# Gate matrices made one token at a time on VectorE and GpSimd, and S of 96 e-tiles computed ahead instead of 64

## The chip, the cores and the metric

The program runs on one core of a Trainium2 chip. TensorE does the matmuls, VectorE (DVE in the rows) and GpSimd (POOL) elementwise work, ScalarE (ACT) activations and copies out of PSUM, SyncE (SP) issues most DMAs; GpSimd also issues the indirect ones. The metric is the device time of one execution in microseconds. The kernel before took 2036.5, 2039.18 and 2039.2 us in three runs, median 2039.18. The profiled execution took 2032.77 us, with a span of 2030.9 us from its first instruction to its last.

## The reference

The block is one layer on 512 tokens of width 1024: adaLN, a dilated-window and a differential attention branch, a merge, and at the end a PEER layer. Only the PEER layer matters here. For every token it picks 128 of 16384 single-neuron experts (8 heads with 16 each, from two top-16 lists of 128 keys) and adds up their outputs:

```
eidx = e1 * PEER_N_KEYS + e2
gate = jax.nn.softmax(top, axis=-1)
u = expert_u[eidx]
vv = expert_v[eidx]
act = jax.nn.gelu(jnp.einsum('td,thkd->thk', xc, u).astype(jnp.float32), approximate=False)
wts = (gate * act).astype(xc.dtype)
return jnp.einsum('thk,thkd->td', wts, vv)
```

## The kernel before

**Two ways for the experts.** The tokens are four groups of 128. Group 0 is done sparsely: for each of its 128 slots one indirect DMA on GpSimd's queue (`gather`, line 1056) brings a row of `expert_u` per token, VectorE takes the dot product (`dot`, line 1062, op at L1064), and a second gather brings the row of `expert_v`, which VectorE adds with its weight (`add`, line 1071, op at L1076). These 256 gathers share four buffers (`GB`), so a gather waits for the VectorE op that frees its buffer. The other three groups, 384 tokens, are done densely over all 16384 experts, in 128 e-tiles of 128 experts.

**Dense path, S.** For an e-tile, `gelu_s` (line 872) loads 512 KB of `uT`, ScalarE makes its rounded part (L91) and VectorE or GpSimd the rest (L92, tile `wlo`), TensorE does 24 matmuls of 384 columns into `pj` (L86 to L88, 8 of each), and ScalarE applies gelu into `am` (L879). The first `NS` e-tiles are done ahead of the main loop by `run_ahead` and stored in DRAM (`gls`); the others are done live, inside the main loop.

**Dense path, gate matrices.** Each of the 384 tokens needs a 128x128 matrix of its gates (16384 experts), which is a product of two one-hot factors. The stage at lines 1092 to 1152 makes it in 96 steps of `T` = 4 tokens, 32 steps for each token group. In a step VectorE compares two index rows with `iota` (`oh0`, `oh1`, L1125), multiplies `oh0` by the high and by the low half of the gates (`og0`, `og1`, L1130), all four as 128x512 operations on f16; TensorE does 8 matmuls with `oh1` (L1137, tile `pg`), two for each token; ScalarE copies the result into `stage` (L1139). After 8 steps four DMAs write it to DRAM (`gd`, L1146). Tiles `oh` and `og` have three buffers each, `pg` two.

**The main loop** (lines 1196 to 1223) goes over the 128 e-tiles in chunks of 8. A chunk of 8 live e-tiles takes turns with a chunk of 8 that were done ahead (order d a d a ...). `stage_s` runs 4 tiles ahead (`LEAD`): it loads `gch`, 1536 KB per chunk from `gd`, and either loads `am` from `gls` (L1168) or computes it. Then VectorE multiplies `am` by the gates (L1201), ScalarE and VectorE split it into `ah` and `al`, the 512 KB of `expert_v` are loaded and split (on GpSimd for one tile in four), and TensorE does 18 matmuls of 512 columns into `y` (L1220). Jobs of the sparse path are handed out along the way; `J0` = 48 of them belong to the gate stage, and a live tile gets twice the share of one done ahead.

**What sets the order.** Each engine works through its own queue in order. The queues come from a scheduler that goes by its own estimates, so instructions of the gate stage, of S and of the sparse jobs are woven together there; GpSimd's main-loop part keeps the order written.

## Time and profile before

| what | value |
|---|---|
| median of three runs | 2039.18 us |
| profiled execution, its span | 2032.77 us, 2030.9 us |
| TensorE busy | 1911.0 us (94%) |
| VectorE busy | 1589.5 us (78%) |
| ScalarE, GpSimd busy | 847.8 us (42%), 854.3 us (42%) |
| attention, projections, first S tiles and selection | 0 to about 923 us |
| gate stage: first `pg` matmul to last | 923.5 to 1213 us |
| TensorE idle until the first `y` matmul | 1213 to 1227 us |
| main loop: first `y` matmul to last | 1227.7 to 2023.5 us |

Busy time is an average over stages, so each stage is read by itself. In a timeline, matmuls overlap and their ends are modelled: the pace is the distance between two starts.

### The profile page before, as it was taken

What the parts mean: (1) busy time and instruction counts of PE and PEld (TensorE: products, weight loads), DVE (VectorE), ACT (ScalarE), POOL (GpSimd) and SP (SyncE); (2) the same over time, 40 slices, a digit from 0 to 9 for tenths busy, and PEclk for the clock granted to TensorE, in tenths of its full rate; (3) what the DMA queues carried; (4) which work ended last, traced back from release to release, by engine and by line L of the source; (5) the groups of instructions that cost most, each with busy time, mean ns of one, the idle gap of its engine ahead of it and who ended that gap; (6) DMA issues with size and microseconds to landing.
All of it is one profiled execution on the core that took longest, in us unless ns stands there. A gap on an engine that the chain in (4) does not pass through costs nothing.

```text
span 2030.9 us, 28280 instructions
## 1 busy us (share of the span) xinstructions
PE 1911.0 (94%) x9858; PEld 1658.5 (82%) x9858; DVE 1589.5 (78%) x3212; ACT 847.8 (42%) x1330; POOL 854.3 (42%) x598
## 2 busy tenths in 40 slices
PE   6999999989899899999999968999999999999998
PEld 5987777777777788999999946888888888888886
DVE  7488585886766669999888885777879797777887
ACT  3444345656533333345555652333333333333331
POOL 2554332352244531021442313465657464646553
PEclk9999999999999899999999958999999999999999
DMA  7344142132146421577788767888888788878886
GB/s 260 94 125 115 53 146 58 37 94 88 54 150 213 142 72 54 163 268 267 277 305 295 253 251 250 296 313 292 320 291 331 283 323 303 307 289 303 308 305 218
DMA packets 197200, 434.71 MB, mean 214 GB/s; under 512 B 16273, under 2 KB 95426, under 8 KB 196930
## 3 DMA queue, kind: packets, MB, share of 16 engines
q1 hardware_dynamic: 159376, 296.55, 43.2%
q0 software_dynamic: 36864, 134.23, 18.2%
q10 hardware_dynamic: 818, 2.12, 0.3%
q8 instruction: 77, 1.26, 0.2%
q14 instruction: 65, 0.53, 0.1%
HBM read 390.90 MB, written 41.94 MB: 213 GB/s over the span
## 4 chain that ended last, share of the span: by engine, by line
PE 47%; DVE 16%; DMA 9%; issue 5%; POOL 1%; ACT 1%; SPq 0%; DVEq 0%; POOLq 0%; ACTq 0%
PE y L1220 18%; PE pj L86 8%; PE pj L87 7%; PE pj L88 7%; PE pg L1137 3%; DMA gat<-expert_u,eidx 2%; DMA gat<-expert_v,eidx 2%; DVE wlo L92 2%; DMA raw<-uT 1%; DMA raw<-w_ada 1%; DVE mr L933 1%; DVE acc L1076 1%; DVE idx L935 1%; DMA raw<-expert_v 1%; DVE oh L1125 1%
## 5 line engine op out<-in xcount | busy, mean ns | idle before, releaser
L91 ACT ACTIVATE whi<-raw 128x1024 fp32r<-128x1024 f32 (+3 forms) x431 | 384.7, 896 | 520.4 <-DMA raw<-expert_v 142.9
L92 POOL TENSOR_TENSOR wlo<-raw,whi 128x1024 fp32r<-128x1024 f32 (+2 forms) x156 | 332.5, 2135 | 557.3 <-ACT whi L91 534.2
L92 DVE TENSOR_TENSOR wlo<-raw,whi 128x1024 fp32r<-128x1024 f32 (+3 forms) x275 | 310.5, 1131 | 115.1 <-ACT whi L91 114.5
L88 PE MATMUL pj<-h2h,wlo 128*128 128x384 f32 x1008 | 344.2, 342 | 4.1 <-DVE wlo L92 4.1
L86 PE MATMUL pj<-h2h,whi 128*128 128x384 f32 x1008 | 343.5, 341 | 0.5 <-ACT am L879 0.5
L87 PE MATMUL pj<-h2l,whi 128*128 128x384 f32 x1008 | 343.3, 341 | 0.0
L1058 POOL DMA_INDIRECT gat<-expert_u,eidx x128 | 162.1, 1266 | 254.9 <-DVE rkt L1015 102.2
L1220 PE MATMUL y<-whi,ah 128*128 128x512 f32 x768 | 248.0, 398 | 16.2 <-ACT ah L91 16.2
L1058 POOL DMA_INDIRECT gat<-expert_v,eidx x128 | 188.9, 1476 | 143.6 <-DVE acc L1076 83.6
L1220 PE MATMUL y<-wlo,ah 128*128 128x512 f32 x768 | 245.4, 397 | 0.0
L1220 PE MATMUL y<-whi,al 128*128 128x512 f32 x768 | 236.1, 398 | 7.8 <-DVE al L92 7.7
L1076 DVE SCALAR_TENSOR_TENSOR acc<-gat,wts,acc 128x1024 f32<-128x1024 f32 x127 | 188.9, 1488 | 43.3 <-DMA gat<-expert_v,eidx 43.0
L86 PE MATMUL pj<-whi,hh 128*128 128x512 f32 (+2 forms) x512 | 190.8, 386 | 10.7 <-DVE gA L651 4.4
L1064 DVE SCALAR_TENSOR_TENSOR gscr<-gat,h2tok 128x1024 bf16<-128x1024 f32 x128 | 176.1, 1376 | 27.3 <-DMA gat<-expert_u,eidx 27.0
L87 PE MATMUL pj<-wlo,hh 128*128 128x512 f32 (+2 forms) x512 | 194.9, 381 | 2.3 <-DVE wlo L92 2.3
L88 PEld LDWEIGHTS pj<-h2h,wlo 128*128 128x128 f32 x1008 | 191.1, 190 | 5.2 <-DVE wlo L92 4.8
L86 PEld LDWEIGHTS pj<-h2h,whi 128*128 128x128 f32 x1008 | 191.0, 190 | 4.5 <-ACT am L879 1.4
L87 PEld LDWEIGHTS pj<-h2l,whi 128*128 128x128 f32 x1008 | 191.0, 189 | 2.5
L88 PE MATMUL pj<-whi,hl 128*128 128x512 f32 (+2 forms) x512 | 190.5, 379 | 0.0
L1220 PEld LDWEIGHTS y<-whi,ah 128*128 128x128 f32 x768 | 144.2, 189 | 46.4 <-ACT ah L91 17.2
L1220 PEld LDWEIGHTS y<-whi,al 128*128 128x128 f32 x768 | 144.2, 189 | 46.4 <-DVE al L92 11.6
L1220 PEld LDWEIGHTS y<-wlo,ah 128*128 128x128 f32 x768 | 145.1, 189 | 35.2
(313 smaller groups left out, 3213.3 us busy)
## 6 DMA issues: line engine op xcount, KB each, us to landing
raw<-uT SPq DMA_DIRECT2D x128, 512.0 KB, 4.3
raw<-expert_v SPq DMA_DIRECT2D x128, 512.0 KB, 5.4
gd<-stage SPq DMA_DIRECT2D x48, 512.0 KB, 5.2
gch<-gd SPq DMA_DIRECT2D x16, 1536.0 KB, 10.9
raw<-w_in SPq DMA_DIRECT2D x88, 256.0 KB, 2.7
raw<-w_ada SPq DMA_DIRECT2D x64, 256.0 KB, 2.9
am<-gls SPq DMA_DIRECT2D x64, 192.0 KB, 8.2
gls<-am SPq DMA_DIRECT2D x62, 192.0 KB, 3.8
```

Source lines behind the costliest of these rows:

```text
L86: nc.tensor.matmul(ps, lh, rh, start=start, stop=False)
L87: nc.tensor.matmul(ps, lh, rl, start=False, stop=False)
L88: nc.tensor.matmul(ps, ll, rh, start=False, stop=stop)
L91: nc.scalar.activation(hi, raw, AF.Copy)
L92: (eng or nc.vector).tensor_tensor(lo, raw, hi.bitcast(F32), op=OP.subtract)
L933: nc.vector.match_replace(out=r, in_to_replace=v[:, 0:8], in_values=s, imm_value=-3.0e38)
L935: nc.vector.max_index(out=i[:, 8:16], in_max=v[:, 8:16], in_values=r)
L1058: nc.gpsimd.indirect_dma_start(out=t, out_offset=None, in_=src, in_offset=bass.IndirectOffsetOnAxis(ap=eidx[:, s:s + 1], axis=0))
L1064: nc.vector.scalar_tensor_tensor(scr, t, 1.0, h2tok, op0=OP.mult, op1=OP.mult, accum_out=act[:, s:s + 1])
L1076: nc.vector.scalar_tensor_tensor(acc, t, wts[:, s:s + 1], acc, op0=OP.mult, op1=OP.add)
L1137: nc.tensor.matmul(p[:, j * 128:j * 128 + 128], oh[1][:, :, q + j], pcs[i][:, :, q + j], start=i == 0, stop=i == 1)
L1220: nc.tensor.matmul(ys[b][n], l[:, bs], r[:, n * 512:n * 512 + 512], start=n_ == 0 and i == 0, stop=n_ == 127 and i == 2)
```

## The change

The value `NS` goes from 64 to 96. In the chunk order this makes one live chunk followed by three done ahead (d a a a, four times). In the gate stage one comparison and two products of a step are replaced by one operation per token and half, which compares `line` (0 to 127) with the token's first index and multiplies by the token's gate half, both taken as one scalar per partition. VectorE does this for the high half, GpSimd for the low half; the results lie contiguously for each token. The second comparison (`oh`) stays as it was.

```
-    ND, NS = 384, 64
+    ND, NS = 384, 96
...
+    line = gt.tile([128, 128], HF, name="line")
+    nc.vector.tensor_copy(line, ioti)
...
-            s = gt.tile([128, 128], HF if n < 2 else F32, name=f"sT{n}", bufs=2)
+            s = gt.tile([128, 128], HF if n == 1 else F32, name=f"sT{n}", bufs=2)
...
+        gh16 = gt.tile([128, 128], HF, name="gh16", bufs=1)
+        nc.vector.tensor_copy(gh16, tr[2])
+        gp = [gt.tile([128, 128], F32, name="gp", bufs=2), tr[2]]
+        nc.vector.tensor_copy(gp[0], gh16)
+        nc.vector.tensor_tensor(gp[1], tr[2], gp[0], op=OP.subtract)
...
-            oh = []
-            for i in range(2):
-                o = gt.tile([128, 128, T], HF, name=f"oh{i}", bufs=OB)
-                nc.vector.tensor_tensor(o, tr[i][:, None, ts].to_broadcast([128, 128, T]), iota, op=OP.is_equal)
-                oh.append(o)
-            pcs = []
-            for i in range(2):
-                o = gt.tile([128, 128, T], HF, name=f"og{i}", bufs=OB)
-                nc.vector.tensor_tensor(
-                    o, oh[0], gp[i][:, None, ts].to_broadcast([128, 128, T]), op=OP.mult)
-                pcs.append(o)
+            oh = gt.tile([128, 128, T], HF, name="oh", bufs=OB)
+            nc.vector.tensor_tensor(oh, tr[1][:, None, ts].to_broadcast([128, 128, T]), iota, op=OP.is_equal)
+            pcs = [gt.tile([128, T, 128], HF, name=f"og{i}", bufs=OB) for i in range(2)]
+            for j in range(T):
+                tj = slice(t0 + j, t0 + j + 1)
+                nc.vector.tensor_scalar(pcs[0][:, j], line, tr[0][:, tj], gp[0][:, tj], op0=OP.is_equal, op1=OP.mult)
+                nc.gpsimd.tensor_scalar(pcs[1][:, j], line, tr[0][:, tj], gp[1][:, tj], op0=OP.is_equal, op1=OP.mult)
...
-                        nc.tensor.matmul(p[:, j * 128:j * 128 + 128], oh[1][:, :, q + j], pcs[i][:, :, q + j],
+                        nc.tensor.matmul(p[:, j * 128:j * 128 + 128], oh[:, :, q + j], pcs[i][:, q + j, :],
```

On TensorE's queue, this is the place before where the last S matmul of the gate stage stands (`pj`), and then the end of the stage:

```order
L86 MATMUL pj<-h2h,whi 128x384
L87 MATMUL pj<-h2l_6198,whi 128x384
L88 MATMUL pj<-h2h,wlo 128x384
L1137 LDWEIGHTS oh_10291
L1137 MATMUL pg<-og_10293,oh_10291 128x128
...
L1137 MATMUL pg<-og_11055,oh_11051 128x128
L1220 MATMUL y_12372<-whi,ah 128x512
```

Behind these rows the matmuls of S have run out, and only gate steps follow up to the first `y`. The same place now (lines after the edit are three lower):

```order
L87 MATMUL pj<-h2l_6198,whi 128x384
L88 MATMUL pj<-h2h,wlo 128x384
L1134 LDWEIGHTS oh
L1134 MATMUL pg<-og_11173,oh 128x128
...
L1134 MATMUL pg<-og_11434,oh 128x128
L1217 MATMUL y_13846<-whi,ah 128x512
```

Before, 26 of the 96 steps stand behind the last S matmul, now 8. In front of the first `pg` matmul stand about 27.5 S tiles before and 28 now; in front of the first `y` matmul 70 before and 102 now (in both, six of them are the first live tiles).

On GpSimd's queue, the end of the gate stage before had only gathers of the sparse path (`gat`) and splits of main-loop weights (`wlo`):

```order
L92 TENSOR_TENSOR wlo_12385<-raw_12387,whi_12386 128x1024
L1058 DMA gat_11067<-expert_u,eidx_8063 128x1024
L92 TENSOR_TENSOR wlo_12451<-raw_12453,whi_12452 128x1024
L92 TENSOR_TENSOR wlo_12519<-raw_12521,whi_12520 128x1024
L1058 DMA gat_12579<-expert_u,eidx_8063 128x1024
```

None of these is waited for by the gate steps. Now the low halves of the last 8 steps (`og1`, four tokens in a row) stand between gathers:

```order
L1058 DMA gat_14194<-expert_v,eidx_8063 128x1024
L1129 TENSOR_SCALAR og1_11203<-line_8074,sT0_10401,sT2_10409 128x128 x4
L1129 TENSOR_SCALAR og1_11225<-line_8074,sT0_10401,sT2_10409 128x128 x4
L1129 TENSOR_SCALAR og1_11250<-line_8074,sT0_10401,sT2_10409 128x128 x4
L1058 DMA gat_14197<-expert_v,eidx_8063 128x1024
L1058 DMA gat_14200<-expert_v,eidx_8063 128x1024
L1129 TENSOR_SCALAR og1_11306<-line_8074,sT0_10401,sT2_10409 128x128 x4
L1129 TENSOR_SCALAR og1_11331<-line_8074,sT0_10401,sT2_10409 128x128 x4
L1058 DMA gat_14265<-expert_v,eidx_8063 128x1024
L1129 TENSOR_SCALAR og1_11353<-line_8074,sT0_10401,sT2_10409 128x128 x4
L1058 DMA gat_14268<-expert_v,eidx_8063 128x1024
L1058 DMA gat_14304<-expert_v,eidx_8063 128x1024
```

Each of these gathers waits for a buffer, and the `og1` behind it waits with it. VectorE's queue over the same 8 steps now reads, in its second half:

```order
L1076 SCALAR_TENSOR_TENSOR acc_8065<-gat_14123,wts_8067,acc_8065 128x1024
L1076 SCALAR_TENSOR_TENSOR acc_8065<-gat_14126,wts_8067,acc_8065 128x1024
L1128 TENSOR_SCALAR og0_11305<-line_8074,sT0_10401,gp_10413 128x128 x4
L1123 TENSOR_TENSOR oh_11303<-sT1_10405,iota_8072 128x512
L1128 TENSOR_SCALAR og0_11330<-line_8074,sT0_10401,gp_10413 128x128 x4
L1123 TENSOR_TENSOR oh_11328<-sT1_10405,iota_8072 128x512
L1076 SCALAR_TENSOR_TENSOR acc_8065<-gat_14129,wts_8067,acc_8065 128x1024
L1128 TENSOR_SCALAR og0_11352<-line_8074,sT0_10401,gp_10413 128x128 x4
L1076 SCALAR_TENSOR_TENSOR acc_8065<-gat_14194,wts_8067,acc_8065 128x1024
L1123 TENSOR_TENSOR oh_11350<-sT1_10405,iota_8072 128x512
L1076 SCALAR_TENSOR_TENSOR acc_8065<-gat_14197,wts_8067,acc_8065 128x1024
L1076 SCALAR_TENSOR_TENSOR acc_8065<-gat_14200,wts_8067,acc_8065 128x1024
```

Before, no add of the sparse path stood between the last 11 steps on VectorE's queue. In the main loop, VectorE's queue has 9 to 11 dots and adds per eight e-tiles of a chunk done ahead before, and now 9 to 13 with one of 17; of a live chunk 15 to 17 before and 17 to 20 now.

## Rows read from the trace of the kernel before

**Rows 1.** The page: TensorE's busy time, and the chain by engine.
```profile
PE 1911.0 (94%) x9858; PEld 1658.5 (82%) x9858; DVE 1589.5 (78%) x3212; ACT 847.8 (42%) x1330; POOL 854.3 (42%) x598
...
PE 47%; DVE 16%; DMA 9%; issue 5%; POOL 1%; ACT 1%; SPq 0%; DVEq 0%; POOLq 0%; ACTq 0%
```

**Rows 2.** Busy time by stretch (start:end length, engines, clock, DMA share, GB/s), gate stage.
```profile
923.00:1130.00 207.00, 207.00 (x1326) 195.66 (x1325) 183.01 (x375) 110.56 (x135) 65.68 (x36) 1.00 0.80 280
1130.00:1213.00 83.00, 68.97 (x476) 60.42 (x473) 74.59 (x172) 52.54 (x55) 26.76 (x14) 0.77 0.71 250
...
1213.00:1227.00 14.00, 0.00 (x0) 0.00 (x0) 0.49 (x2) 0.33 (x1) 0.00 (x0) 0.50 0.93 311
```

**Rows 3.** The same stretches, line L1137 alone (TensorE, its loads).
```profile
1130.00:1213.00 83.00, 46.46 (x332) 35.91 (x329) 0.77 0.71 250
923.00:1130.00 207.00, 64.69 (x439) 45.73 (x440) 1.00 0.80 280
```

**Rows 4.** The same stretches, line L86 alone, 8 matmuls per S tile.
```profile
1130.00:1213.00 83.00, 16.68 (x48) 9.22 (x48) 0.77 0.71 250
923.00:1130.00 207.00, 100.62 (x293) 55.68 (x293) 1.00 0.80 280
```

**Rows 5.** Timeline of TensorE in S (start, length, instruction).
```profile
1119.52 0.34 PE L86 MATMUL pj<-h2h,whi 128*128 128x384 f32 x1
...
1120.56 0.34 PE L86 MATMUL pj<-h2h,whi 128*128 128x384 f32 x1
```

**Rows 6.** Timeline of VectorE near the end of the gate stage.
```profile
1198.47 1.78 DVE L1125 TENSOR_TENSOR oh<-sT,iota 128x512 f16<-128x512 f16 x5
1200.14 1.45 DVE L1130 TENSOR_TENSOR og<-oh,gp 128x512 f16<-128x512 f16 x4
```

**Rows 7.** Groups by form: 128x128 operations with scalars (busy, mean ns, idle before).
```profile
L349 POOL TENSOR_SCALAR ropeS<-ropeS 128x128 f32<-128x128 f32 x4 | 1.1, 296 | 0.0
...
L757 POOL TENSOR_SCALAR ob<-ob,r 128x128 f32<-128x128 f32 x8 | 3.8, 491 | 6.3 <-DVE r L103 6.3
...
L1015 DVE TENSOR_SCALAR rkt<-rb 128x128 f32<-128x128 bf16 x4 | 0.9, 214 | 0.0
```

**Rows 8.** Timelines of GpSimd and VectorE in the main loop.
```profile
1481.90 3.57 POOL L92 TENSOR_TENSOR wlo<-raw,whi 128x1024 fp32r<-128x1024 f32 x1
...
1483.11 3.44 DVE L1076 SCALAR_TENSOR_TENSOR acc<-gat,wts,acc 128x1024 f32<-128x1024 f32 x1
...
1488.08 1.27 DVE L1076 SCALAR_TENSOR_TENSOR acc<-gat,wts,acc 128x1024 f32<-128x1024 f32 x1
```

**Rows 9.** Busy time by stretch in the main loop, columns as in rows 2.
```profile
1296.00:1328.00 32.00, 32.00 (x163) 29.05 (x162) 20.72 (x25) 11.74 (x16) 17.46 (x9) 1.00 0.72 269
...
1353.00:1386.00 33.00, 33.00 (x144) 26.61 (x143) 26.72 (x28) 10.97 (x15) 20.90 (x12) 1.00 0.99 364
...
1759.00:1795.00 36.00, 34.54 (x150) 27.71 (x150) 31.07 (x39) 12.21 (x16) 17.55 (x14) 1.00 0.99 369
...
1780.00:1790.00 10.00, 10.00 (x45) 8.04 (x44) 8.75 (x12) 4.12 (x5) 4.77 (x4) 1.00 1.04 402
```

**Rows 10.** One of these stretches, line L1220 alone.
```profile
1353.00:1386.00 33.00, 32.81 (x142) 26.25 (x141) 1.00 0.99 364
```

**Rows 11.** DMA issues (KB each, median us to landing).
```profile
raw<-expert_v SPq DMA_DIRECT2D x128, 512.0 KB, 5.4
...
gch<-gd SPq DMA_DIRECT2D x16, 1536.0 KB, 10.9
...
am<-gls SPq DMA_DIRECT2D x64, 192.0 KB, 8.2
...
gat<-expert_v,eidx POOLq DMA_INDIRECT x128, 7.4
```

**Rows 12.** VectorE's waits, 1250 to 2000 us (total, times, longest).
```profile
DVE acc L1076 <- DMA gat<-expert_v,eidx: 43.0, 27, 5.1
...
DVE am L1201 <- DMA am<-gls: 19.7, 8, 4.9
```

**Rows 13.** The page: the gathers' issue on GpSimd.
```profile
L1058 POOL DMA_INDIRECT gat<-expert_v,eidx x128 | 188.9, 1476 | 143.6 <-DVE acc L1076 83.6 <-DVE gscr L1064 22.7 <-DVE acc L1074 10.0
```

More of the change, by code (lines that the diff above doesn't have):

```diff
@@ L1105, in peer @@
             nc.tensor.transpose(p[:, :128], t, ident)
-            s = gt.tile([128, 128], HF if n < 2 else F32, name=f"sT{n}", bufs=2)
+            s = gt.tile([128, 128], HF if n == 1 else F32, name=f"sT{n}", bufs=2)
             nc.scalar.activation(s, p[:, :128], AF.Copy, scale=1.0 if n < 2 else GS)
             tr.append(s)
-        gT = tr[2]
-        gp = []
-        for i in range(2):
-            q = gt.tile([128, 128], HF, name=f"gp{i}", bufs=2)
-            nc.vector.tensor_copy(q, gT)
-            if i == 0:
-                nc.vector.tensor_tensor(gT, gT, q, op=OP.subtract)
-            gp.append(q)
+        gh16 = gt.tile([128, 128], HF, name="gh16", bufs=1)
[3 more added lines that the diff above has]
+        nc.vector.tensor_tensor(gp[1], tr[2], gp[0], op=OP.subtract)
         for t0 in range(0, 128, T):
@@ L1121, in peer @@
                 st = gt.tile([128, 128, 32], F32, name="stage", bufs=SB)
-            oh = []
-            for i in range(2):
-                o = gt.tile([128, 128, T], HF, name=f"oh{i}", bufs=OB)
-                nc.vector.tensor_tensor(o, tr[i][:, None, ts].to_broadcast([128, 128, T]), iota, op=OP.is_equal)
-                oh.append(o)
-            pcs = []
-            for i in range(2):
-                o = gt.tile([128, 128, T], HF, name=f"og{i}", bufs=OB)
-                nc.vector.tensor_tensor(
-                    o, oh[0], gp[i][:, None, ts].to_broadcast([128, 128, T]), op=OP.mult)
-                pcs.append(o)
+            oh = gt.tile([128, 128, T], HF, name="oh", bufs=OB)
[5 more added lines that the diff above has]
+                nc.gpsimd.tensor_scalar(pcs[1][:, j], line, tr[0][:, tj], gp[1][:, tj], op0=OP.is_equal, op1=OP.mult)
             for q in range(0, T, 4):
```

## The prediction

> **What bounds the kernel now.** I read the page first: TensorE is busy 94% of the span and has the largest share of the chain that ended last, 47% [rows 1]. Then busy time by stretch. From 923 to 1130 us, in the gate stage, TensorE is busy for all of 207 us; from 1130 to 1213 for 69 of 83 at a granted clock of 0.77, while VectorE is busy for 75; then it idles 14 us until the first y matmul [rows 2]. In the main loop it is full around live chunks and loses a little in chunks done ahead [rows 9]. So the questions are what the end of the gate stage costs, and whether the main loop stays with TensorE.
>
> Paces at full clock. S matmuls start 0.173 us apart (six steps in 1.04 us) [rows 5], so an S tile of 24 takes 4.16 us. In the full 207 us stood 293/8 = 36.6 S tiles [rows 4], 152 us, and 439/8 = 54.9 gate steps [rows 3]; the other 55 us make 1.00 us a step. The y matmuls: 142 in 33 us [rows 10], 0.232 us, 4.18 us for the 18 of a tile.
>
> **The end of the gate stage.** Between 1130 and 1213 us TensorE did 48/8 = 6.0 S tiles and 332/8 = 41.5 steps [rows 3, 4], work for 25 + 41.5 = 66.5 us. Lost: 16.5 us. There S has run out and the steps go at VectorE's pace: five operations start within 1.67 us, 0.335 each, four to a step, 1.34 us, with sparse adds between [rows 6].
>
> **The main loop.** 128 y tiles by 4.18 and 128 - 70 = 58 S tiles by 4.16 make 776 us. It lasts from 1227.7 to 2023.5, 796 us, so 20 us are lost, and the stretches in question show where: 1.5 us in the 36 us of one chunk done ahead [rows 9], of which there are eight, 12 us in all; the rest at the first and last tiles.
>
> **The change, part by part.**
>
> *S tiles moved.* 32 S tiles (32 by 4.16 = 133 us of TensorE) go from the main loop into the gate stage. TensorE is full in both, so this alone is worth nothing. Each takes along its 512 KB load and its split, mostly on VectorE, and adds a store and a load of 192 KB.
>
> *VectorE's part of a step.* Removed are three operations of 0.335 us, 1.0 us; added are four on 128 elements. The trace has no such f16 operation with two scalars. From above, a 128x128 operation with immediates took 214 ns [rows 7]; from below, a quarter of 335 ns is 84 ns, with nothing fixed [rows 6]. So 0.34 to 0.86 us a step; I take 0.5, in between, as neither row has its form. This gives no time by itself, since VectorE is not what TensorE waits for while S lasts; it cuts the pace of the last steps from 1.34 to about 0.84.
>
> *GpSimd's part.* Four operations on 128x128: 296 ns where GpSimd was alone and 491 where VectorE worked on the same tile [rows 7], 1.2 to 2.0 us a step, below the 4.1 to 5.0 us that a step with its 0.75 to 0.97 S tiles takes on TensorE. GpSimd was busy 66 of 207 us [rows 2], so it has room. I take 0.35 us. It could be much slower if the two scalars or f16 cost extra; that is left to a rival.
>
> *TensorE's reads.* `og` is now read contiguously. The step costs 1.00 us for 8 matmuls, 125 ns each. No row shows the same matmul with contiguous reads; if they save a tenth, 96 steps give 10 us, if nothing, 0. I take 0, since the matrix that is loaded for each matmul (`oh`) keeps its layout, and keep the 10 for the range.
>
> *The new tail.* Behind the last S matmul stand 8 steps instead of 26, work for 8 us. But low halves now share GpSimd's queue with gathers, and a gather that waits for its buffer holds them up. Along the queues shown: VectorE does two adds, 2 by 1.27 us [rows 8]; two gathers wait for these, and land 7.4 us after their issue [rows 11]; VectorE adds both, 2.5 us; the last two low halves each stand behind another gather, twice 1.48 us [rows 13] and four operations of 0.35; then the last matmuls, 1 us. Sum: 2.5 + 7.4 + 2.5 + 5.8 + 1.0 = 19 us against 8. Lost: 11 us. From both sides: 0, if the three buffers of `oh` and `og` let both engines run ahead far enough; 20, if nothing overlaps and the first gathers wait too. I take 11: the tail gives 16.5 - 11 = 5.5 us. The 14 us without TensorE that follow stay, since `gch` still waits for the last `gd` write and takes 10.9 us to land [rows 11].
>
> *The main loop with three chunks ahead in a row.* A tile done ahead moves 512 + 192 + 192 KB [rows 11] and its gathers: 10 to 11 per eight tiles before, 1.61 MB with them, which at 4.18 us a tile is 384 GB/s. In 10 us with TensorE full 402 GB/s were moved [rows 9]. VectorE's new queue has mostly 9 to 12 per eight tiles: 1.51 to 1.70 MB, 361 to 407 GB/s. So the demand is about what it was, only 24 tiles long instead of 8. What was lost came with the step from a live chunk to one ahead; of these steps there are now four, 4 by 1.5 = 6 us, and for the eight further chunks I take a third of that each, 4 us. 10 us instead of 12: the main loop gives 2 us. From both sides: 8 us if a long stretch loses nothing after its first tiles; or a loss, see below.
>
> **The sum.** -5.5 - 2 = -7.5 us on a span of 2030.9, and on its execution's 2032.8: 2025.3. That execution lies 6.4 us under the median of the three runs, 2039.2, so on that footing **2032 us**, with an own range of 2020 to 2044.
>
> **The rivals.**
>
> *DMA holds up the long stretches (slower).* In the chunks done ahead the DMA share was already 0.99 at 364 and 369 GB/s over 33 and 36 us [rows 9], and VectorE waited for gathers 27 times, 43 us, and for `am` 8 times, 20 us [rows 12]. If 364 is what lasts, a tile of 1.60 MB takes 4.40 us instead of 4.18, and 84 of the 96 tiles (all but the first three of each stretch) lose 0.22, 18 us; with 6 us at the four steps that is 24 against 12 now, and with the tail's gain 2039 + 12 - 5.5 = 2046. It decides from 381 GB/s down, where a tile of 1.60 MB falls behind TensorE. Against it: 402 GB/s in the middle of such a stretch [rows 9]. The Trainium skill (HBM Reference, Specifications (TRN2)) gives a core about 358 GB/s as its share of a domain, and about 425 when it streams alone; the trace's 402 speaks for the second. By 358 a tile would take 4.47 us and the time would come to 2052.
>
> *VectorE and GpSimd shut each other out (slower).* In the main loop an add that takes 1.27 us took 3.44 while GpSimd had a split of 3.57 us under way, and ended only after it [rows 8]. In the new gate stage VectorE has 74 splits and 45 sparse operations (by its queue) of 1.27 us, some 16 us of selection (183 us of the 207, less 55 steps by 1.34 and 37 splits and 37 sparse operations by 1.27 [rows 2, 6, 8]), and 96 steps by 0.67 to 1.19: 231 to 281 us. If none of GpSimd's 384 operations can lie beside any of these, 114 to 188 us are added: 345 to 469, against 74 by 4.16 plus 96, 404 us on TensorE. At my own values it is 167 + 80 + 134 = 381, just below. It decides from an operation of 0.41 us on GpSimd, and costs 20 us at 0.46: about 2052; up to 2097 at 0.491 and the slow VectorE value. The Trainium skill (GPSIMD Engine Reference, section 8, Key points) says that GpSimd shares its SBUF interfaces with VectorE and contends with operations of two SBUF inputs or in a two-port mode. The held add agrees; whether one-input operations on 128 elements do the same, the trace hardly shows.
>
> *Tail and boundaries go altogether (faster).* If the last 8 steps are hidden and long stretches lose nothing: -16.5 - 8, 2015; with cheaper reads of `og` down to 2005. For it: VectorE's pace of 0.84 is under TensorE's 1.00. Against it: the gathers in GpSimd's queue.
>
> *It only moves work (no change).* The tail on GpSimd costs what VectorE's cost, and the main loop loses its 20 us as now: 2039.
>
> **How the numbers follow.** Chances: forecast 0.40, DMA 0.22, shutting out 0.13, all gone 0.15, only moved 0.10. About 0.2% (4 us) is what can be told from no change. Faster, under 2035: 0.65 of the forecast, all of the fast rival, little of the rest, 0.46. Within: a quarter of the forecast, half of only moved, a quarter of DMA, 0.22. Slower: most of the two slow rivals, 0.32. The range leaves out the fastest reads and the upper half of shutting out: 2010 to 2062.
>
> **What would show it.** In the new profile: TensorE full from 925 us to the last S at about 1321, and behind it a tail of about 19 us for 8 steps; GpSimd's new operation near 0.35 us and VectorE's near 0.12; the first y 14 us after the last step; 128 y tiles in 128 by 4.18 + 26 by 4.16 + about 18 = 661 us. It is wrong if TensorE waits for `og` while S still lasts, if the chunks done ahead run at more than 4.3 us a tile beyond their first three, or if the tail takes over 28 us.

## The result and the profile after

The changed kernel takes 2148.07 us (median of 4 runs, 2136.9 to 2153.3) beside 2037.84 for the kernel before on the same chip: ratio 1.056, 95% interval 1.053 to 1.059. It is slower; 2032 with a range of 2010 to 2062 was forecast. The profiled execution took 2153.29 us, its span is 2151.5.

The page answers to [rows 1]. First come busy us (share, instructions) of each engine, then three lines of its 40 slices of 54 us (busy tenths; PEclk is the granted clock, 9 for 90% of full speed or more):

```profile
PE 1935.4 (90%) x9858; PEld 1628.7 (76%) x9858; DVE 1588.7 (74%) x3325; ACT 846.1 (39%) x1330; POOL 1183.9 (55%) x966
...
PE   6999998998999998988889999539999999899888
...
POOL 2553331531355230289999999944455555646444
PEclk9999999999999999999999999759999999999999
```

GpSimd (POOL) rose from 854 to 1184 us, and an eight and eight nines fill its slices 18 to 26, 914 to 1399 us: the gate stage, which lasts from 928 to 1422 us. TensorE has no gap there of the length of a slice until the stage's end. By stretch, answering to [rows 2] (until the last S matmul, the tail, the wait for the first y; columns as there):

```profile
928.00:1130.00 202.00, 168.39 (x988) 143.56 (x987) 141.39 (x296) 78.23 (x100) 195.71 (x157) 0.95 0.65 218
1130.00:1372.00 242.00, 235.29 (x1502) 196.68 (x1502) 145.88 (x331) 120.16 (x144) 240.58 (x233) 0.99 0.59 200
1372.00:1422.00 50.00, 12.83 (x66) 6.75 (x65) 22.62 (x40) 9.30 (x9) 47.55 (x45) 0.55 0.53 178
1422.00:1441.00 19.00, 0.66 (x2) 0.39 (x2) 4.19 (x6) 2.04 (x3) 1.03 (x1) 0.50 0.85 267
```

The fifth busy column is GpSimd: 195.7 of 202, 240.6 of 242, 47.6 of 50 us. VectorE, the third, has room everywhere. What GpSimd does from 928 to 1422 us (groups of instructions: count | busy, mean ns | idle before):

```profile
L1129 POOL TENSOR_SCALAR og<-line,sT,sT 128x128 f16<-128x128 f16 x383 | 419.8, 1107 | 1.5
L1058 POOL DMA_INDIRECT gat<-expert_v,eidx x27 | 32.0, 1185 | 5.1 <-issue 4.5 <-DVE og L1128 0.5 <-DMA gat<-expert_v,eidx 0.2
L1058 POOL DMA_INDIRECT gat<-expert_u,eidx x18 | 19.7, 1092 | 3.5 <-issue 3.2 <-DVE gp L1115 0.3
L92 POOL TENSOR_TENSOR wlo<-raw,whi 128x1024 fp32r<-128x1024 f32 x5 | 13.2, 2638 | 0.0
```

The low halves take 1.107 us each, not 0.35; with gathers and five splits that makes 485 of the 494 us. TensorE's waits there (total, times, longest) end on them, and 39.6 of the 71.2 us fall before 1372 us, while S still lasts:

```profile
PE pg L1134 <- POOL og L1129: 71.2, 83, 10.1
```

What GpSimd does in the tail, 1372 to 1422 us, in the same columns:

```profile
L1129 POOL TENSOR_SCALAR og<-line,sT,sT 128x128 f16<-128x128 f16 x33 | 32.4, 988 | 0.2
L1058 POOL DMA_INDIRECT gat<-expert_v,eidx x10 | 11.0, 1099 | 2.2 <-issue 2.0 <-DMA gat<-expert_v,eidx 0.2
L92 POOL TENSOR_TENSOR wlo<-raw,whi 128x1024 fp32r<-128x1024 f32 x2 | 4.7, 2344 | 0.0
```

Contrary to the reading of the queue under "The change", gathers hardly wait for a buffer here: GpSimd is idle for 2.2 us before ten of them. The tail is GpSimd's own work: 32 us of low halves for the last 8 steps, 11 us of issuing gathers and 5 us of two splits. TensorE's longest wait, 10.1 us, is the one for the first low half behind both splits and four gathers.

**Where the 120 us are.** For every kernel below I counted S tiles from the matmul starts and took off the work at the paces that the prediction had found, 4.16 us for an S tile, 1.00 for a gate step, 4.18 for a y tile. What is left of a stage is "lost". The main loop counts from the first y matmul to the last. The 1.00 us of a gate step is that of the old layout of `og`; where the new one is used (changed, e1, e3, e4, e8, e9, e12) a step costs TensorE less, as the last rows of the experiments show, and more than listed is lost in the gate stage.

| kernel | first gate step to first y, us | S tiles in it | lost | main loop, us | S tiles in it | lost |
|---|---|---|---|---|---|---|
| before | 304.3 | 42.5 | 32 | 796.0 | 58 | 20 |
| changed | 512.5 | 74 | 109 | 702.6 | 26 | 59 |
| e1 gate operations alone | 474.7 | 42 | 204 | 801.5 | 58 | 25 |
| e2 96 ahead alone | 391.4 | 71.5 | -2 | 709.8 | 29 | 54 |
| e3 both halves on VectorE | 429.6 | 71 | 38 | 717.8 | 29 | 62 |
| e4 the same, 64 ahead | 356.3 | 42 | 86 | 801.3 | 58 | 25 |
| e5 96 ahead, splits on VectorE | 391.4 | 71.5 | -2 | 686.8 | 29 | 31 |
| e6 96 ahead, jobs moved | 391.4 | 71.5 | -2 | 692.5 | 29 | 37 |
| e7 64 ahead, jobs moved | 302.6 | 42.5 | 30 | 804.1 | 58 | 28 |
| e8 changed, splits on VectorE | 513.8 | 74 | 110 | 676.9 | 26 | 34 |
| e9 changed, low half by ratio | 418.3 | 71 | 27 | 723.8 | 29 | 68 |
| e10 e5 and e6 together | 391.4 | 71.5 | -2 | 691.5 | 29 | 36 |
| e11 e5 with 88 jobs early | 409.6 | 73.5 | 8 | 660.1 | 27 | 13 |
| e12 changed, one-input split | 485.4 | 76.8 | 70 | 698.3 | 26 | 55 |
| e13 e11 with 64 ahead | 329.5 | 42.5 | 57 | 802.2 | 58 | 26 |
| e14 e11 with 128 jobs early | 407.8 | 73.5 | 6 | 716.8 | 27 | 69 |

Changed against before, by these paces: 77 us more lost in the gate stage and 39 in the main loop, 116 of the 120.6 by which the span grew. The first gate step also comes 4.6 us later. So two causes are to be found.

### The profile page after: what moved, and what is told of

Same layout as the page of the kernel before. It is cut to its first block, busy times and chain, and to the rows that moved or that the text cites. A ratio compares the mean times of both kernels' runs of the same rounds, so it can differ in the third digit from the quotient of the medians.

```text
span 2151.5 us, 28938 instructions
## 1 busy us (share of the span) xinstructions
PE 1935.4 (90%) x9858; PEld 1628.7 (76%) x9858; DVE 1588.7 (74%) x3325; ACT 846.1 (39%) x1330; POOL 1183.9 (55%) x966
## 3 DMA queue, kind: packets, MB, share of 16 engines
q8 instruction: 77, 1.26, 0.2%
## 5 line engine op out<-in xcount | busy, mean ns | idle before, releaser
L92 POOL TENSOR_TENSOR wlo<-raw,whi 128x1024 fp32r<-128x1024 f32 (+2 forms) x140 | 270.2, 1934 | 356.5 <-ACT whi L91 329.3
L1129 POOL TENSOR_SCALAR og<-line,sT,sT 128x128 f16<-128x128 f16 x384 | 420.7, 1106 | 2.4 <-DVE sT L1116 0.9
L92 DVE TENSOR_TENSOR wlo<-raw,whi 128x1024 fp32r<-128x1024 f32 (+3 forms) x291 | 322.5, 1111 | 99.6 <-ACT whi L91 98.7
L88 PE MATMUL pj<-h2h,wlo 128*128 128x384 f32 x1008 | 355.2, 352 | 8.8 <-POOL wlo L92 4.6
L86 PE MATMUL pj<-h2h,whi 128*128 128x384 f32 x1008 | 356.5, 354 | 3.0 <-ACT am L879 3.0
L87 PE MATMUL pj<-h2l,whi 128*128 128x384 f32 x1008 | 357.1, 354 | 0.0
L1217 PE MATMUL y<-whi,ah 128*128 128x512 f32 x768 | 234.1, 400 | 23.0 <-ACT ah L91 19.9
L1058 POOL DMA_INDIRECT gat<-expert_v,eidx x128 | 166.3, 1299 | 118.3 <-DVE acc L1076 76.3
L86 PEld LDWEIGHTS pj<-h2h,whi 128*128 128x128 f32 x1008 | 194.6, 193 | 9.2 <-issue 3.9
L86 PE MATMUL pj<-whi,hh 128*128 128x512 f32 (+2 forms) x512 | 192.8, 389 | 9.5 <-DVE gA L651 4.4
L1134 PE MATMUL pg<-og,oh 128*128 128x128 f16 x768 | 127.4, 237 | 77.5 <-POOL og L1129 71.6
L91 ACT ACTIVATE ah<-am 128x384 fp32r<-128x384 f32 x128 | 67.0, 524 | 324.9 <-PE y L1217 205.6
```

The costliest lines, as they stand in the source:

```text
L86: nc.tensor.matmul(ps, lh, rh, start=start, stop=False)
L87: nc.tensor.matmul(ps, lh, rl, start=False, stop=False)
L88: nc.tensor.matmul(ps, ll, rh, start=False, stop=stop)
L91: nc.scalar.activation(hi, raw, AF.Copy)
L92: (eng or nc.vector).tensor_tensor(lo, raw, hi.bitcast(F32), op=OP.subtract)
L1058: nc.gpsimd.indirect_dma_start(out=t, out_offset=None, in_=src, in_offset=bass.IndirectOffsetOnAxis(ap=eidx[:, s:s + 1], axis=0))
```

## The experiments

Ratios are against the kernel before, run beside on the same chip, with 95% intervals.

**e1 and e2: each half of the change alone.** e1 is the changed kernel with one number back, e2 the kernel before with one number changed.

```
e1  -    ND, NS = 384, 96
    +    ND, NS = 384, 64
e2  -    ND, NS = 384, 64
    +    ND, NS = 384, 96
```

> The new gate operations with 64 e-tiles of S ahead, as before. Theory G (GpSimd's 384 operations are the bound of the gate stage): they take as long as in the changed kernel, 384 by 0.79 to 1.11 us = 303 to 425 us, while TensorE has only 42 S tiles and 96 steps there, 272 us; so the stage, 304 us from first step to first y before, becomes 330 to 440, and the main loop keeps its 796: 2065 to 2175, likeliest 2150. Rival N (the long stretches of tiles done ahead are what costs): within 10 us of the kernel before, about 2040.

> The kernel before with 96 e-tiles of S ahead and its old gate operations. Theory G: what was lost in the main loop of the changed kernel (703 us against 663) comes from GpSimd's late queue and goes, so the time is 2030 to 2045. Rival N: three chunks done ahead in a row cost the 40 us by themselves, through their loads and gathers: the main loop takes about 700 us and the time is about 2080.

e1: 2210.2 us, 1.086 (1.081 to 1.091). e2: 2043.7, 1.003 (1.001 to 1.005). The gate operations alone are worse than the whole change: with 42 S tiles TensorE has only 271 us of work to lay over GpSimd's, with 74 it has 404. e1 came out above its range: beside 389 us of gate operations GpSimd had 61 us of gathers and splits in that stage, which I had left out. e2 met the time of theory G, but not for its reason: it gained 34 us in the gate stage and lost as many in the main loop. Theory G fell for the main loop; its loss comes with the 96 tiles and not with the new operations. The gate stage of e2, 925 to 1317 us, columns as above:

```profile
925.00:1317.00 392.00, 392.00 (x2496) 376.30 (x2495) 274.30 (x565) 203.29 (x248) 70.01 (x39) 1.00 0.73 253
```

TensorE is full for all of it at a clock of 1.00, the level of 2.4 GHz: the old 26 steps of tail are hidden beneath S tiles.

**e3 and e4: both halves on VectorE, with 96 and with 64 tiles ahead.**

```
-                nc.gpsimd.tensor_scalar(pcs[1][:, j], line, tr[0][:, tj], gp[1][:, tj], ...
+                nc.vector.tensor_scalar(pcs[1][:, j], line, tr[0][:, tj], gp[1][:, tj], ...
```

> The changed kernel with the low halves on VectorE too; GpSimd has no gate work. Theory G: no GpSimd bound is left; VectorE has 96 steps of 8 by 0.25 to 0.31 plus 0.43 us, 233 to 280 us, beside 167 us of splits, sparse adds and selection, 400 to 447 against TensorE's 404; the gate stage loses 10 to 50 us, the main loop at most 10: 2045 to 2095. Rival N: main loop as in the changed kernel, 40 us lost there, on top of whatever the gate stage loses: 2085 or more.

> As the kernel with both halves on VectorE, but 64 e-tiles ahead. VectorE has 233 to 280 us of steps and about 110 us of splits, adds and selection, 343 to 390, against TensorE's 272: the gate stage takes 40 to 85 us longer than before's 304, the main loop 796 as before: 2075 to 2125 under both theories; if instead VectorE's small operations cost only 0.12 us as I took, 96 steps take 133 us and the time is within 10 us of before.

e3: 2090.4, 1.028 (1.023 to 1.034). e4: 2090.0, 1.026 (1.022 to 1.031). Both times fell into their first ranges, but e3's main loop lost 62 us, 42 more than before, as rival N had it. Without GpSimd 58 of the changed kernel's us come back. Of what is left the main loop's part comes with the 96 tiles, as in e2; in the gate stage, where e3 loses 40 us more than e2, it is VectorE's: in e4 it is busy for 311 of the 326 us up to the last step, and first step to first y takes 52 us longer than with the old four operations. So VectorE's one does not cost 0.12 us either. It lasts 0.305 us in the row of e3, and most starts lie 0.223 us apart:

```profile
L1128 DVE TENSOR_SCALAR og<-line,sT,gp 128x128 f16<-128x128 f16 x384 | 113.8, 305 | 6.8 <-PE pg L1134 6.8
```

**m1 and m2: the operation by itself.** Series of 24 equal operations on GpSimd, VectorE idle; then both engines together.

> No part of the layer is computed; the kernel runs only series of small operations, first GpSimd alone (eight forms on 128 rows), then VectorE alone (three forms), then both beside each other. Theory F (the form of the operation is what costs): GpSimd alone needs 0.79 us for the f16 operation with two scalars from SBUF, and about 0.3 us for at least one of its relatives (f32; one scalar; immediates; two tensors), which names the property that costs. Theory C (contention makes most of it): alone 0.3 to 0.5 us in this series, 0.8 and more only beside VectorE. Beside VectorE's 128x1024 f32 operation with two inputs I expect 1.6 to 2.0 us under both, beside its operation with two scalars no change. VectorE's own two-scalar operation alone: 0.24 to 0.31 us.

> No part of the layer is computed; a second series of small operations on GpSimd, alone, then beside VectorE. If a comparison costs by itself about 0.3 us and a scalar from SBUF about 0.3: one scalar, multiply 0.59; two scalars, multiply and add 0.75 or less if only the first scalar costs; comparison with an immediate, 0.6; multiplication with an immediate 0.2 to 0.3. With 512 elements, immediates and multiply and add: 0.7 to 0.9. Beside VectorE's 128x1024 f32 two-input operation the cheap form (0.30 us alone) is held as long as the other one was, 3.5 us, if it is held until VectorE ends and a number of times that goes by its length; about 1.3 us if the holding grows with the operation's own length. Beside VectorE's one-input 128x1024 f32 operation, 0.79 to 0.95.

GpSimd alone in m1, in this order: the changed kernel's form; the same in f32; one scalar, comparison alone; comparison and multiplication with immediates; multiplication and addition with immediates; the changed form on 512 elements; multiplication of two tensors.

```profile
L70 POOL TENSOR_SCALAR a<-line,line,gate 128x128 f16<-128x128 f16 x24 | 18.7, 791 | 3.5 <-DVE gate L55 3.5
L72 POOL TENSOR_SCALAR a<-line,gate 128x128 f32<-128x128 f32 x24 | 18.6, 791 | 0.0
L74 POOL TENSOR_SCALAR a<-line,line 128x128 f16<-128x128 f16 x24 | 13.9, 603 | 0.0
L76 POOL TENSOR_SCALAR a<-line 128x128 f16<-128x128 f16 x24 | 14.6, 642 | 0.0
L78 POOL TENSOR_SCALAR a<-line 128x128 f16<-128x128 f16 x24 | 6.4, 300 | 0.0
L80 POOL TENSOR_SCALAR w<-line,line,gate 128x512 f16<-128x512 f16 x24 | 49.4, 2073 | 0.0
L82 POOL TENSOR_TENSOR a<-line,hot 128x128 f16<-128x128 f16 x24 | 9.3, 427 | 0.0
```

And in m2: one scalar, multiplication alone; two scalars, multiplication and addition; an immediate, comparison alone; an immediate, multiplication alone; on 512 elements, with immediates, multiplication and addition, then comparison and multiplication.

```profile
L70 POOL TENSOR_SCALAR a<-line,gate 128x128 f16<-128x128 f16 x24 | 14.0, 602 | 3.7 <-DVE gate L55 3.7
L72 POOL TENSOR_SCALAR a<-line,line,gate 128x128 f16<-128x128 f16 x24 | 10.4, 452 | 0.0
L74 POOL TENSOR_SCALAR a<-line 128x128 f16<-128x128 f16 x24 | 11.9, 533 | 0.0
L76 POOL TENSOR_SCALAR a<-line 128x128 f16<-128x128 f16 x24 | 11.9, 534 | 0.0
L78 POOL TENSOR_SCALAR w<-line 128x512 f16<-128x512 f16 x24 | 14.1, 625 | 0.0
L80 POOL TENSOR_SCALAR w<-line 128x512 f16<-128x512 f16 x24 | 45.4, 1928 | 0.0
```

Multiplication with addition is a fast case, 0.300 us; a comparison with a multiplication takes 0.642, and either of the two alone 0.53. Two scalars from SBUF add 0.15, one adds 0.07. For the changed form f16 or f32 makes no difference. My expectation for m2 that the parts add up was wrong: a lone multiplication costs as much as a lone comparison.

Beside VectorE (all from the stretch in which VectorE's series runs): m1 beside 128x1024 f32 with two inputs, beside VectorE's two-scalar operation, beside the 128x512 comparison.

```profile
L98 POOL TENSOR_SCALAR a<-line,line,gate 128x128 f16<-128x128 f16 x17 | 56.8, 3354 | 0.0
L96 DVE TENSOR_TENSOR d<-r,z 128x1024 f32<-128x1024 f32 x48 | 56.0, 1243 | 0.0
...
L104 POOL TENSOR_SCALAR a<-line,line,gate 128x128 f16<-128x128 f16 x25 | 22.3, 905 | 0.0
...
L110 POOL TENSOR_SCALAR a<-line,line,gate 128x128 f16<-128x128 f16 x17 | 23.5, 1396 | 0.0
```

m2: the fast case beside 128x1024 f32 with two inputs, then the changed form beside 128x1024 f32 with one input.

```profile
L87 POOL TENSOR_SCALAR a<-line 128x128 f16<-128x128 f16 x46 | 56.6, 1261 | 0.0
...
L93 POOL TENSOR_SCALAR a<-line,line,gate 128x128 f16<-128x128 f16 x17 | 42.1, 2491 | 0.0
L91 DVE TENSOR_SCALAR d<-r 128x1024 f32<-128x1024 f32 x63 | 40.8, 724 | 0.0
```

The 0.79 us become 3.4 beside two inputs (I had expected 2.0 at most) and 2.5 beside one (expected 0.95 at most), and 0.9 beside VectorE's two-scalar operation, where I had expected no change. The fast case's 0.30 become 1.26, as expected if the holding up grows with the operation's own length. VectorE pays little: its two-input starts lie 1.17 to 1.23 us apart instead of 1.14. So both theories hold something: the form makes 0.79 of 0.35, and VectorE makes 1.11 of it. An estimate says that VectorE's work is enough for that. Beside two-input f32 work GpSimd does 0.79 us of its own in 3.5, so it loses 0.77 of that time. These are VectorE's splits and sparse operations in the changed kernel from 928 to 1422 us:

```profile
L92 DVE TENSOR_TENSOR wlo<-raw,whi 128x1024 fp32r<-128x1024 f32 x72 | 89.2, 1241 | 33.9 <-ACT whi L91 33.8
L1076 DVE SCALAR_TENSOR_TENSOR acc<-gat,wts,acc 128x1024 f32<-128x1024 f32 x25 | 32.6, 1304 | 28.3 <-DMA gat<-expert_v,eidx 28.3
L1064 DVE SCALAR_TENSOR_TENSOR gscr<-gat,h2tok 128x1024 bf16<-128x1024 f32 x22 | 27.8, 1262 | 19.0 <-DMA gat<-expert_u,eidx 19.0
```

They are busy for 150 us, of which GpSimd would lose 115; its 384 operations, at 1.106 us instead of 0.791, took 121 us longer.

**e9 and e12: each of the two taken away in the kernel.** In e9 GpSimd multiplies the high half by one scalar; in e12 VectorE's splits for S tiles done ahead have one input, which leaves out the low part of those weights and the wait for ScalarE's rounded part. Dots stand for lines not shown.

```
e9  +        rat = gt.tile([128, 128], F32, name="rat", bufs=2)
    +        nc.vector.tensor_scalar(rat, gp[0], 1e-6, None, op0=OP.max)
    +        nc.vector.reciprocal(rat, rat)
    +        nc.vector.tensor_tensor(rat, rat, gp[1], op=OP.mult)
    ...
    -                nc.gpsimd.tensor_scalar(pcs[1][:, j], line, tr[0][:, tj], gp[1][:, tj], op0=OP.is_equal, op1=OP.mult)
    +                nc.gpsimd.tensor_scalar(pcs[1][:, j], pcs[0][:, j], rat[:, tj], None, op0=OP.mult)
e12 +        if ahead and eng is nc.vector:
    +            nc.scalar.activation(hi, raw, AF.Copy)
    +            nc.vector.tensor_scalar(lo, raw, 0.0, None, op0=OP.mult)
    ...
```

> The changed kernel, but GpSimd makes the low half from the high half, by one multiplication with a scalar (low gate by high gate), without a comparison and with one scalar. Theory F (comparison and second scalar make the operation slow; alone the series showed 0.64 us for a comparison with immediates against 0.30 without, and 0.79 with two scalars): 0.40 to 0.50 us alone, 0.5 to 0.75 beside VectorE, 384 of them 190 to 290 us, below TensorE's 404: the gate stage falls from 512 to 405 to 440 us and the time to 2040 to 2080. Rival C (VectorE shuts GpSimd out, whatever the form): operations keep a mean near 1 us, since most of them would wait for VectorE's two-input operations; gate stage above 470, time above 2105.

> The changed kernel, but for the S tiles of the gate stage VectorE does not subtract: wlo is raw times 0, an operation with one input tensor (the low part of the weights is left out of S there). Theory C (VectorE's two-input operations hold GpSimd up; of 420 us in the gate operations 302 are the operation alone, 118 the holding): its mean falls from 1.106 to 0.88 to 0.98 us, GpSimd's work in the stage from 485 to 400 to 440 us, the stage from 512 to 425 to 465, the time to 2060 to 2105. Theory F alone (the form, whatever runs beside it): mean 1.05 or more, stage above 490, time above 2125.

e9: 2083.6, 1.022 (1.019 to 1.025). e12: 2111.8, 1.038 (1.034 to 1.041). GpSimd's gate operation in e9, then in e12:

```profile
L1133 POOL TENSOR_SCALAR og<-og,rat 128x128 f16<-128x128 f16 x384 | 330.5, 874 | 1.1
```

```profile
L1133 POOL TENSOR_SCALAR og<-line,sT,sT 128x128 f16<-128x128 f16 x384 | 389.7, 1024 | 5.3 <-PE pg L1138 2.9
```

In e9 the gate stage loses 27 us instead of 109: the form is most of what these two edits give back, though the operation got shorter by less than I expected (0.874, not 0.75 at most; alone it took 0.602 in m2), and the time lies just above its range. In e12 the loss falls to 70, so VectorE's splits matter. The mean of 1.024, the stage of 485 us and the time all lie between the ranges of theories C and F, so neither was met, and m2 says why: an operation with one input holds GpSimd up as well. By an estimate as above, its splits of 49 us at 0.69 lost (0.79 us in 2.6) cost GpSimd 34 us instead of 69, and its operations fell by 31. Neither edit takes its cause away whole, so the shares of the two are known only roughly.

**e5, e6, e7, e10: the main loop.** First what a stall is. GpSimd, then VectorE, in e2 at the second tile of a stretch ahead, where y waits 8.0 us for GpSimd's `wlo`:

```profile
1555.04 1.01 POOL L1058 DMA_INDIRECT gat<-expert_v,eidx  x1 [8.69 <-DVE acc L1076]
1556.70 3.28 POOL L1058 DMA_INDIRECT gat<-expert_v,eidx  x1 [0.65 <-DVE acc L1076]
1560.01 3.96 POOL L92 TENSOR_TENSOR wlo<-raw,whi 128x1024 fp32r<-128x1024 f32 x1
```

```profile
1553.01 0.56 DVE L1201 TENSOR_TENSOR am<-am,gch 128x384 f32<-128x384 f32 x1 [6.29 <-DMA am<-gls]
1553.49 1.28 DVE L1076 SCALAR_TENSOR_TENSOR acc<-gat,wts,acc 128x1024 f32<-128x1024 f32 x1
```

`am` lands late and VectorE's queue stops for 6.3 us; the sparse add stands behind it, two gathers wait for adds, and the split of `expert_v` stands behind both gathers. There are three such stalls, of 6.7 to 8.0 us, 22.6 of the 28.2 us that y waits for `wlo`. The loads were dense before this one:

```profile
1540.00:1552.00 12.00, 12.00 (x53) 9.63 (x52) 3.96 (x5) 2.10 (x3) 2.65 (x3) 1.00 1.05 390
```

Two edits of e2 cut this chain in different places; e10 has both, and e7 is the edit of e6 with 64 tiles ahead:

```
e5  -        split(vh, vl, raw, nc.gpsimd if e % 4 == 1 else nc.vector)
    +        split(vh, vl, raw, nc.gpsimd if e % 4 == 1 and e >= NS else nc.vector)
e6  -        done += (njobs - J0) * (1 if e < NS else 2) / (254.0 - NS)
    +        live = n_ + LEAD < 128 and order[n_ + LEAD] >= NS
    +        done += (njobs - J0) * (2 if live else 1) / (250.0 - NS)
```

> The kernel before with 96 e-tiles ahead, and in the main loop the splits of expert_v for tiles done ahead all on VectorE (GpSimd keeps those of live tiles). Theory Q (GpSimd's splits, queued behind gathers, make the stalls of the long stretches): the 28 us that y waits for GpSimd's wlo go, the main loop falls from 710 to 680 to 690 us, the time to about 2020. Theory D (the loads make them: at the step from live to ahead am arrives late, and VectorE's acc, the gathers and the split only follow): the stalls stay and end on am or VectorE instead, main loop 700 to 720, time 2035 to 2055.

> The kernel before with 96 e-tiles ahead; the double share of sparse jobs goes to the iterations in which a live tile's S is staged (four tiles earlier), not to those whose own tile is live. Theory D: in the last four live tiles a double share of gathers meets y matmuls without S, some 590 GB/s of demand, and the stall of 7 to 8 us at the first tiles ahead pays for it; with the share moved, most of three such stalls go: main loop 710 to about 685, time about 2020. Theory Q: as many gathers stand before the same splits, so within 8 us of the unmoved one, 2036 to 2052.

> The kernel before, only with the share of sparse jobs moved by four tiles. Theory D: it loses 20 us in the main loop, at eight steps from live to ahead; half of it goes, 2026 to 2032. Theory Q: within 6 us of before.

> The kernel before with 96 e-tiles ahead, the splits of expert_v for tiles done ahead on VectorE and the sparse jobs moved by four tiles. Each edit alone gave 17 to 23 us in the main loop. If they cure two different things, the main loop falls from 687 and 692 to 670 to 678 and the time to 2003 to 2012; if both cure the same wait (the split behind gathers), it stays at 685 to 692 and the time at 2015 to 2025.

e5: 2021.2, 0.992 (0.990 to 0.995). e6: 2019.0, 0.991 (0.988 to 0.995). e7: 2044.2, 1.004 (1.002 to 1.006), some 8 us slower than before, so neither theory D's gain nor within theory Q's 6 us. e10: 2020.4, 0.993 (0.990 to 0.995). With 96 ahead each edit alone brings some 20 us, both together no more: they cure the same wait. e5 came out as theory Q had it, e6 as theory D had it; in e6 y waits 10.1 us for GpSimd's `wlo` instead of 28.2. That e7 gains nothing says that the place of the jobs is not at fault as such: with 64 ahead, in the kernel before and in e7, y never waits for GpSimd's `wlo`, so there is no such wait to shorten. TensorE's waits in the main loop, e2 and then e5 (after the bar: idle before, and what ended it):

```profile
L1220 PE MATMUL y<-wlo,ah 128*128 128x512 f32 x762 | 245.0, 404 | 28.2 <-POOL wlo L92 28.2
```

```profile
L1220 PE MATMUL y<-wlo,ah 128*128 128x512 f32 x762 | 242.6, 397 | 8.4 <-DVE wlo L92 8.4
```

The loads set no lower pace: in e2 a whole chunk ahead runs at 4.20 us a tile with TensorE full, at a DMA share of 0.98 and 358 GB/s:

```profile
1777.00:1811.00 34.00, 34.00 (x147) 27.34 (x146) 28.61 (x34) 12.61 (x17) 17.30 (x12) 1.00 0.98 358
```

**e8: the same edit in the changed kernel.** One line, as e5.

> The changed kernel with one more edit: in the main loop, the splits of expert_v for tiles done ahead on VectorE. If the changed kernel's main loop (703 us, 40 over what I expected) loses through the same GpSimd queue as the kernel with 96 e-tiles alone (710 to 687 with this edit), its main loop falls to 675 to 690 and the time to 2120 to 2138; the gate stage stays at 512 us. Rival: what is lost there comes from the late end of GpSimd's gate work, then the main loop stays at 695 to 710 and the time at 2140 to 2155.

2135.4, 1.047 (1.044 to 1.051), as expected first. Main loop 702.6 to 676.9, gate stage unchanged. So 26 of the 39 us that the changed kernel lost more in its main loop came through GpSimd's splits there, a loss that the 96 tiles bring with the old gate operations as well.

**e11, e13, e14: more sparse jobs in the gate stage.** e11 is e5 with J0 = 88 instead of 48, e13 the same with 64 tiles ahead, e14 e11 with J0 = 128.

> The kernel before with 96 e-tiles ahead, the splits of expert_v for tiles done ahead on VectorE, and 88 of the 264 sparse jobs in the gate stage, not 48. The gate stage lost nothing with 96 tiles ahead (391 us for 393 us of TensorE work) and VectorE is busy for 297 of its 391 us, so 40 more jobs (about 50 us of VectorE, 20 MB of loads) should fit at a cost of 0 to 10 us. If loads and gathers are what the main loop still loses to (687 against 656 of TensorE work), it gains 10 to 20 us: 2003 to 2015; if the jobs hinder the gate stage's weave, 2020 to 2035.

> The kernel before (64 e-tiles ahead), with the splits of expert_v for tiles done ahead on VectorE and 88 sparse jobs in the gate stage. If the gain of the same edits with 96 ahead (2001) needs the longer gate stage, which hides its own tail, this one stays at 2020 to 2045: 31 us are lost in its gate stage, and more with 40 more jobs on VectorE. If the two edits alone do it, 2000 to 2012.

> 96 e-tiles ahead, splits of expert_v for tiles done ahead on VectorE, 128 jobs in the gate stage instead of 88. With 88 its main loop took 675 us for 656 of TensorE work, so at most 15 us more are to be had: 1990 to 2003 if the gate stage still loses nothing; above 2005 if its VectorE and DMA now hold up the S tiles.

e11: 2001.2, 0.983 (0.980 to 0.986), just below its range of 2003 to 2015, faster than both kernels and the best of all; it keeps the old gate operations. e13: 2065.2, 1.015 (1.012 to 1.019): without the longer gate stage the jobs cost it 25 us there, more than I had expected, so the gain needs the 96 tiles. e14: 2057.2, 1.011 (1.008 to 1.015), a miss, and not through the gate stage, which lost 6 us: 93 gathers had been issued by its first y, hardly more than e11's 90, so the rest of the 128 stood ahead of a split in GpSimd's queue, and one wait held up the first chunk:

```profile
PE y L1220 <- POOL wlo L92: 57.2, 1, 57.2
```

**TensorE's reads of `og`, from the kept traces.** No run changed the layout alone, but the matmuls of the gate steps can be compared: the same shape and type, `oh` laid out as before, and `og` read with four tokens interleaved before and contiguously after. Eight in a row between two S matmuls, before and then in e3, at S's pace of 0.17 us on either side:

```profile
965.24 0.34 PE L86 MATMUL pj<-h2h,whi 128*128 128x384 f32 x1
965.42 1.10 PE L1137 MATMUL pg<-og,oh 128*128 128x128 f16 x8
966.28 0.43 PE L87 MATMUL pj<-h2l,whi 128*128 128x384 f32 x1
...
1062.61 0.34 PE L86 MATMUL pj<-h2h,whi 128*128 128x384 f32 x1
1062.79 0.64 PE L1134 MATMUL pg<-og,oh 128*128 128x128 f16 x8
1063.23 0.42 PE L87 MATMUL pj<-h2l,whi 128*128 128x384 f32 x1
```

From S to S it is 1.04 us before and 0.62 in e3, so the eight cost 0.87 us and 0.45. In the changed kernel they mostly stand in pairs, which cost 0.06 us each. Over 96 steps that is some 40 us less for TensorE (an estimate from these rows), which no kernel here turned into time: in none with the new layout is TensorE busy throughout the gate stage.

## Why the prediction was wrong

**What bounds, and the paces: right for the old layout of `og`.** e2 has 391.4 us for 393 of S tiles and steps, and undisturbed chunks ahead take 33.6 us, 4.20 a tile.

**GpSimd's part: the step that failed.** "I take 0.35 us", from the 296 and 491 ns of [rows 7]. The 296 belong to an operation of the same size that multiplies and adds immediates (-1.0 and 0.0), the one fast case (0.300 in m1). The 491, read as VectorE's doing, belong to the same pair of operations with one scalar from SBUF, and their median is 0.446 us; m2 has the pair with two scalars at 0.452 with VectorE idle. So neither row had a comparison in it, and both were of the fast pair; the changed form takes 0.791 alone and 1.106 in the kernel. 384 by 0.791 are 304 us, with 65 of gathers and splits 369, a little under the forecast's 404 for TensorE and about even with it when the cheaper reads of `og` are taken off; the 121 us of holding up bring it to 490 (485 measured). e9 and e12 show in the kernel that each of the two matters, and of these edits the one of the form gave more.

**VectorE and GpSimd shut each other out, given 0.13: the right kind of mechanism, sized wrongly.** Its upper end of 2097 stopped at 0.491 us an operation. Its sum also let nothing lie beside VectorE: with 0.791 it would have made 231 to 281 + 304 = 535 to 585 us, more than the 494 measured. Beside VectorE GpSimd gets on slowly, but it does. In this stage the one side pays: GpSimd waits, VectorE hardly. That is not so for every pair: beside GpSimd's split VectorE's sparse add is held up in the main loop [rows 8]. The Trainium skill (GPSIMD Engine Reference, section 8, Key points) names VectorE operations with two SBUF inputs or in a two-port mode. The runs agree for two inputs (3.4 us instead of 0.79), and show that one f32 input does it too (2.5); whether that operation ran in a two-port mode, no run here shows.

**VectorE's part.** 0.12 us an operation was forecast, between a distance of starts (84 ns) and a duration (214 ns); the distance of starts is 0.223 in e3, above both, so a step takes 1.2 us of VectorE and not 0.84. That cost no time in the changed kernel, whose VectorE had room, but it ruins e4.

**The tail.** Forecast 19 us, with gathers that wait for buffers as its price; it took 50 (1372 to 1422), and GpSimd's own work was the price. All three signs of being wrong came: this one, TensorE's waits for `og` while S lasted, and, in the changed kernel's main loop, beyond the first three tiles of a stretch ahead, 4.6 us a tile in two of the four stretches (4.3 in the others). The first y came 18.6 us after the last step, not 14.

**S tiles moved: "worth nothing".** In sum right (e2: 1.003), made up of two things that were not seen: the longer stage hides the old tail (34 us), and the main loop loses 34.

**The main loop, "gives 2 us": lost 39 instead.** The rival that DMA holds up long stretches said 2046, and e2 came to 2043.7, but by another road: not a lower pace throughout (undisturbed chunks run at 4.20 us a tile) but chiefly three stalls of 7 to 8 us, in which one late `am` passes through VectorE's sparse operations and the gathers to a split in GpSimd's queue. Why `am` is late there is not settled: the loads were dense before it, at 390 GB/s, but no run took one of them away alone. With the split elsewhere TensorE no longer waits for GpSimd.

**TensorE's reads of `og`, put at nothing** because `oh` keeps its layout, with 10 us kept for the range: by the traces they take about half, some 40 us less in 96 steps. This gain was hidden behind GpSimd.

## What to carry to other kernels

Price a GpSimd operation by its form, not its size alone: the ALU operations, their number and the source of the scalars moved 128x128 from 0.30 to 0.79 us, and VectorE beside it stretched that more than fourfold. Work moved to an engine with idle time also joins its queue, and what stands behind it there (a split behind gathers) may be what TensorE waits for. Where one number moves work between stages, look at what each stage hides: 96 tiles ahead were worth nothing until two cheap edits let the main loop keep up, and then 1.7%. And look in the trace for a gain that another loss hides, as the reads of `og` were here.

## What the hardware showed beyond expectation

- On GpSimd, a comparison with a multiplication costs 1.928 us for 512 elements and 0.642 for 128, 3.3 ns an element of a row; a multiplication with an addition 0.625 and 0.300, 0.85 ns.
- Beside steady work of VectorE, a GpSimd operation of 0.79 us lasts about three of VectorE's two-input f32 operations, and about four of its others: 3.51 us with starts 1.17 apart, 2.59 with 0.65, 1.43 with 0.36, 0.91 with 0.22 (those that lie wholly beside them).
- VectorE's two-scalar f16 operation on 128 elements takes 0.32 us and starts every 0.22 alone; in the kernel it takes 0.305 (e3) to 0.39 (changed).
- A matmul of 128 f16 columns took 0.11 us where its moving tensor was read at every fourth element, and 0.056 where it was contiguous, eight in a row at a granted clock of 1.00.
